# Moving modulation groups between two engines at the norm boundaries, and a reordered opening, in a two-layer diffusion backbone on one core

## The chip, the cores and the metric

The kernel runs on one core of one Trainium2 chip. The metric is the device time of one execution in microseconds (us); the time before is the median of three runs. A profiled execution was recorded beside them: its trace gives every instruction's start and length, what a waiting engine waited for, and the clock that TensorE was granted.

TensorE (PE in the profile) does the matrix products, VectorE (DVE) and ScalarE (ACT) the elementwise work, SyncE (SP) issues the DMA transfers. Each engine runs its instructions in the order in which they stand; the engines wait for each other by semaphores.

## The reference, cut to what matters

The kernel computes one step of a backbone with two layers on 640 tokens (512 latent tokens and 128 prompt tokens), model width 1024, feed-forward width 2816, in fp32. A layer is: feed-forward, mixer (even layer: retention and spatial gating; odd layer: differential attention), feed-forward. Each of these six phases starts with an RMS norm and is modulated:

```
mod = (silu(cond) @ ada_w[i] + ada_b[i]).reshape(-1, 9, 1024)[:, :, None, :]
h = modulate(rms_norm(x, norm_g[i, 0]), mod[:, 0], mod[:, 1])      # h * (1 + scale) + shift
x = x + 0.5 * mod[:, 2] * swiglu(h, ffn_w_in[i, 0], ffn_w_out[i, 0])
h = modulate(rms_norm(x, norm_g[i, 1]), mod[:, 3], mod[:, 4])
out = even_mixer(h, ...) or odd_mixer(h, ...)
x = x + mod[:, 5] * out
h = modulate(rms_norm(x, norm_g[i, 2]), mod[:, 6], mod[:, 7])
x = x + 0.5 * mod[:, 8] * swiglu(h, ffn_w_in[i, 1], ffn_w_out[i, 1])
...
return rms_norm(x, final_norm), ...
```

`swiglu` multiplies by `w_in` (1024 x 5632), takes silu(gate) times up, and multiplies by `w_out` (2816 x 1024). There are two conditions, one for the latent and one for the prompt tokens, so `mod` is a product of two vectors with a matrix of 1024 x 9216 for each layer: nine chunks of 1024 values, numbered 0 to 8.

## The kernel before, in words

**Layout.** The tokens are kept transposed: `xs` holds 8 tiles of 128 features x 640 tokens. All products work on two halves of 320 tokens, "hf 0" and "hf 1". An fp32 operand is split into a high and a low part (suffixes h and l, or `whi` and `wlo` for weights), and each 128x128 weight tile by 320 tokens takes three matmuls: high by high, low activation by high weight, high activation by low weight (lines 707, 708 and 709).

**Weights.** All weights come in groups of 1 MB, in one list called `order`, which SyncE loads one after the other into two buffers (`raw`). A buffer can be loaded again when its group has been used. For a weight group ScalarE writes `whi` (line 320) and VectorE `wlo` = raw - whi (line 321), in two pieces each. The groups are: `fin` (the feed-forward's input weights, 22 groups a phase, worked in chunks of 6, 8 and 8, and after each chunk the output weights), `fout` (four output groups after each chunk), `ein`/`eout` and `oin`/`oout` (the mixers'), and `ada` (modulation, 36 per layer, 4 per chunk). The first `NG0` `fin` groups of a phase are plain (96 matmuls), the others use Strassen's seven products (84 matmuls, with four additions on VectorE for each, lines 299 to 302, and further operand tiles that `tbuild` makes).

**Modulation groups** need no split. On TensorE a group is eight matmuls of 32x256 (`ada`, line 459, two of them joined in `order`'s rows at the opening), and a finished chunk is copied by VectorE (line 469) and turned by transposes (line 472). On VectorE a group is four multiply-and-sum passes of 128x1024 (`ada_v`, line 416 for layer 0, line 418 for layer 1). The set `ADV` lists the groups that go to VectorE. A group runs when the code comes to it in `order`: `next_group`, which fetches the next weights, runs all modulation groups that stand ahead of them (lines 395 to 397), and `mid_ada` starts a VectorE group between two steps of an output projection. The function `weave` (line 223) builds `order`: it puts one modulation group behind each weight group that isn't `fin`, and so-called pads, TensorE groups, ahead of chosen `fin` groups (`FA`).

**The norm boundary.** Where one phase ends and the next begins, the last two output groups are computed for hf 0 and then for hf 1 (`out_proj`, line 822; the odd mixer has its own version). After each product VectorE updates `xs` (line 818), ScalarE squares it (`nq`, lines 532 and 536), VectorE sums the squares (line 540). Then comes a chain for each half: TensorE sums over the features (`n?p`, line 555), VectorE computes a reciprocal square root in ten or so small instructions (from `n?m`, line 559) and spreads it on diagonals (`n?d`, line 564), TensorE broadcasts it to all partitions (`n?b`, line 567), and VectorE and ScalarE write the normed and modulated operands (`H?h`, `H?l`; in one tile with both parts `H?p`, line 626). In the names n10 to n50 the first digit is the phase that begins, the second the half. The first two `fin` groups of the next phase are computed for hf 0 first and then for hf 1 (`first_pair`, line 770). The boundaries in time: into the even mixer (about 457 us), into layer 0's second feed-forward (723), into layer 1's first (1183), into the odd mixer (1633), into layer 1's second feed-forward (1986).

**The opening.** The first norm works on the loaded `x`: ScalarE squares eight tiles, VectorE adds them up in seven additions, five matmuls of 128x1 (`n0p`, line 1553) sum over the features. Around them stand the modulation groups of chunks 0 and 1, whose results the first operands need, and warm-up matmuls (`wu`). The first two `fin` groups run in `first_wide`, whose order is a string of letters, `SQ`: a and b are modulation groups, T finishes their chunks, F readies an operand tile, W fetches the second group's weights and splits two weight pieces, G and g are products with the first and the second group.

```
SQ = 'abGTGFabGTGFWaGbGTFggggGGgggg'
    def weave(ws, ads, pads=(), fins=(), skip=()):
        ...
            if ads and w[0] != "fin" and not (w[0] == "ein" and w[1] < 2) and w[3:] not in skip:
                r.append(ads.pop(0))
    def next_group(key):
        while order[st["i"]][0] == "ada":
            next_ada()
```

## Time and profile before

| | |
|---|---|
| time before, median of 3 runs | 2453.66 us (2453.34 to 2454.06) |
| the profiled execution's own time | 2454.91 us |
| its span in the trace | 2453.1 us |
| mean granted TensorE clock | 0.991 of full speed |
| TensorE busy | 2391.2 us, 97% |
| VectorE busy | 1818.8 us, 74% |
| ScalarE busy | 1065.3 us, 43% |
| GpSimd busy | 53.0 us, 2% |
| moved by DMA | 259.32 MB, 106 GB/s on average |

The span runs from the first to the last instruction in the trace; the execution's own time lies 1.8 us above it. The busy time of an engine leaves out register, branch, semaphore and DMA-issuing instructions. In the timeline's rows the first number is the start in us, the second the length, then engine, line, operation, output and inputs; brackets hold the engine's idle time just before and what ended it. Matmuls are pipelined, so that two neighbouring ones overlap in these rows; how fast they follow each other is read from their starts.

### The profile page before, as it was taken

How to read it: one execution, taken by the hardware profiler on the slowest of the kernel's cores; microseconds unless marked ns; L12 is line 12 of the kernel's file. 1: busy time of each engine (PE TensorE's matmuls, PEld its weight loads, DVE VectorE, ACT ScalarE, POOL GpSimd, SP SyncE). 2: the span in 40 equal slices, each digit the busy share in tenths (PEclk: the TensorE clock that was granted, in tenths of full speed). 3: DMA queues.
4: the chain of work that ended last, by engine and by line, in shares of the span. 5: the costliest groups of instructions: out<-in, count | busy, mean ns of one | idle time of the engine just before them, and what ended most of it. 6: DMA issues, size and time to landing. Idle time of an engine off the chain costs nothing.

```text
span 2453.1 us, 40798 instructions
## 1 busy us (share of the span) xinstructions
PE 2391.2 (97%) x16596; PEld 2337.1 (95%) x16596; DVE 1818.8 (74%) x3723; ACT 1065.3 (43%) x2018; POOL 53.0 (2%) x82
## 2 busy tenths in 40 slices
PE   7999999999999999999999999999999999999998
PEld 6899999899999999999999999999999989999998
DVE  7677767877978777667967775779788877574664
ACT  5425345333325344243543423436767645252442
POOL 0000000000000000000000000001011000000000
PEclk9999999999999999999999999999999999999999
DMA  7332423323241423333223342332111112222121
GB/s 270 133 142 86 155 74 114 138 93 131 93 149 52 155 94 134 134 120 138 104 95 120 130 155 104 136 124 75 43 43 58 55 35 74 82 87 87 69 104 43
DMA packets 44476, 259.32 MB, mean 106 GB/s; under 512 B 5888, under 2 KB 8576, under 8 KB 16768
## 3 DMA queue, kind: packets, MB, share of 16 engines
q1 hardware_dynamic: 41024, 252.37, 28.7%
q8 instruction: 130, 2.13, 0.4%
q0 software_dynamic: 1280, 2.62, 0.3%
q10 hardware_dynamic: 1984, 1.72, 0.2%
q14 instruction: 58, 0.48, 0.1%
HBM read 252.76 MB, written 3.93 MB: 105 GB/s over the span
## 4 chain that ended last, share of the span: by engine, by line
PE 80%; DVE 10%; DMA 4%; ACT 3%; issue 1%; POOL 0%; POOLq 0%; ACTq 0%; DVEq 0%
PE op L707 8%; PE op L708 8%; PE op L709 8%; PE pu L707 7%; PE pu L709 6%; PE pu L708 6%; PE pf L707 3%; PE pf L708 3%; PE pg L709 3%; PE pf L709 3%; PE pg L707 3%; PE pg L708 3%; DVE wlo L321 3%; DMA raw<-in_w_fin 3%; ACT whi L320 2%
## 5 line engine op out<-in xcount | busy, mean ns | idle before, releaser
L321 DVE TENSOR_TENSOR wlo<-raw,whi 128x1024 fp32r<-128x1024 f32 (+1 forms) x484 | 534.0, 1119 | 297.9 <-ACT whi L320 295.8
L320 ACT ACTIVATE whi<-raw 128x1024 fp32r<-128x1024 f32 (+2 forms) x483 | 462.4, 975 | 612.2 <-PE op L708 137.9
L818 DVE SCALAR_TENSOR_TENSOR xs<-op,mod,xs 128x128 f32<-128x128 f32 (+2 forms) x312 | 124.2, 434 | 111.9 <-PE op L709 111.6
L416 DVE SCALAR_TENSOR_TENSOR raw<-raw,sb 128x1024 f32<-128x1024 f32 x72 | 87.4, 1219 | 0.6
L536 ACT ACTIVATE nq<-xs 128x320 f32<-128x320 f32 x84 | 38.6, 467 | 112.3 <-DVE xs L818 110.7
L707 PE MATMUL oq<-H4h,whi 128*128 128x320 f32 x256 | 81.1, 318 | 0.2 <-ACT ov L1015 0.2
L709 PE MATMUL oq<-H4h,wlo 128*128 128x320 f32 x256 | 79.6, 311 | 0.0
L708 PE MATMUL oq<-H4l,whi 128*128 128x320 f32 x256 | 79.3, 310 | 0.0
L1352 DVE TENSOR_REDUCE amx<-as 128x1 f32<-128x320 f32 x144 | 61.6, 460 | 19.2 <-PE as L1348 18.8
L418 DVE CUSTOM_DVE_ANT_0 raw<-raw,sb 128x1024 f32<-128x1024 f32 x60 | 72.9, 1220 | 0.7
L1360 ACT ACTIVATE ap<-as,anm 128x320 f32<-128x320 f32 x128 | 66.2, 531 | 14.1 <-DVE anm L1355 13.9
L905 ACT COPY p<-pg 128x320 f32<-128x320 f32 x76 | 32.4, 426 | 57.9 <-PE pg L709 57.8
L708 PE MATMUL pf<-H3p,whi 128*128 128x320 f32 x172 | 54.4, 318 | 1.8 <-DVE H3p L626 1.8
L708 PE MATMUL pf<-H5p,whi 128*128 128x320 f32 x172 | 53.7, 313 | 2.0 <-DVE H5p L626 2.0
L708 PE MATMUL pf<-H2p,whi 128*128 128x320 f32 x172 | 53.5, 313 | 1.8 <-DVE H2p L626 1.8
L707 PE MATMUL pf<-H3p,whi 128*128 128x320 f32 x172 | 54.5, 320 | 0.0
L709 PE MATMUL pf<-H3p,wlo 128*128 128x320 f32 x172 | 54.2, 316 | 0.0
L707 PE MATMUL pf<-H5p,whi 128*128 128x320 f32 x172 | 53.9, 317 | 0.0
L707 PE MATMUL pf<-H2p,whi 128*128 128x320 f32 x172 | 53.8, 316 | 0.0
L707 PE MATMUL pf<-H0p,whi 128*128 128x320 f32 x172 | 53.6, 314 | 0.0
L709 PE MATMUL pf<-H5p,wlo 128*128 128x320 f32 x172 | 53.4, 312 | 0.0
L301 DVE TENSOR_TENSOR raw<-raw 128x512 f32<-128x512 f32 x76 | 52.3, 688 | 1.5
(2691 smaller groups left out, 8805.0 us busy)
## 6 DMA issues: line engine op xcount, KB each, us to landing
raw<-in_w_fin SPq DMA_DIRECT2D x88, 1024.0 KB, 4.7
raw<-in_ada_w SPq DMA_DIRECT2D x64, 1024.0 KB, 4.8
raw<-in_w_fout SPq DMA_DIRECT2D x32, 1024.0 KB, 4.8
raw<-in_w_fout SPq DMA_DIRECT2D x16, 768.0 KB, 4.2
raw<-in_w_oin SPq DMA_DIRECT2D x12, 1024.0 KB, 4.8
raw<-in_w_ein SPq DMA_DIRECT2D x10, 1024.0 KB, 4.8
raw<-in_ada_w SPq DMA_DIRECT2D x32, 256.0 KB, 6.4
raw<-in_w_eout SPq DMA_DIRECT2D x4, 1024.0 KB, 4.9
```

Source lines behind the costliest of these rows:

```text
L301: sub.tensor_tensor(out=a11, in0=a22, in1=a11, op=ALU.subtract)
L320: S.activation(out=hf, in_=t, func=AF.Copy)
L321: sub.tensor_tensor(out=lf, in0=t, in1=hf.bitcast(F32), op=ALU.subtract)
L416: V.scalar_tensor_tensor(out=o, in0=w, scalar=1.0, in1=sb[:, c * D:(c + 1) * D], op0=ALU.mult, op1=ALU.mult, accum_out=r)
L418: V.tensor_tensor_reduce(out=o, in0=w, in1=sb[:, c * D:(c + 1) * D], scale=1.0, scalar=0.0, op0=ALU.mult, op1=ALU.add, accum_out=r)
L536: S.activation(out=q[:, :n], in_=x[k][:, t0:t1], func=AF.Square)
L707: PE.matmul(o, wh, xh, start=start, stop=False, skip_group_check=more)
L708: PE.matmul(o, wh, xl, start=False, stop=False, skip_group_check=more)
L709: PE.matmul(o, wl, xh, start=False, stop=stop, skip_group_check=more)
L818: V.scalar_tensor_tensor(out=x[m][:, a:b], in0=ps[:, a - t0:b - t0], scalar=mod[:, l, gmod * KD + m, c:c + 1], in1=x[m][:, a:b], op0=ALU.m ...
L1352: V.tensor_reduce(out=mx[:, j, a:a + 1], in_=sps[j][a][:, 0:w], axis=AX.X, op=ALU.max, negate=True)
L1360: S.activation(out=pj[j][:, a * 320:a * 320 + w], in_=sps[j][a][:, 0:w], func=AF.Exp, bias=b, accum_out=(sm[:, j, a:a + 1] if full else s2 ...
```

## The change

*Opening.* A new `SQ` has four new letters. h and i are the two token halves of what G did in one. s splits one weight piece (W no longer splits two). E hands the first group's sums to VectorE and ScalarE and starts `tbuild` as soon as the first group's products are done; before, that stood behind the second group's first half. `NQ = 5` leaves the squares of tiles 5, 6 and 7 out of VectorE's additions (four in place of seven); TensorE sums them, with 20 `n0p` matmuls in place of 5, and a reduction on VectorE adds the four columns. Layer 0's first feed-forward has four plain `fin` groups in place of three.

*Modulation.* Chunks 5 and 8 of layer 0, eight groups, go from VectorE to TensorE. `joined` puts four TensorE groups at the front of a phase, two ahead of its first weights and two behind its second: layer 0's chunk 5 at the even mixer, its chunk 8 at layer 0's second feed-forward, layer 1's chunk 2 at layer 1's first, and layer 1's chunk 8 at layer 1's second. The new `pe_adas` runs the first two between hf 0 and hf 1 of the last two output groups, and the other two between hf 0 and hf 1 of the new phase's first two groups. Layer 1's chunks 2 and 8 were among the pads before; `FA` shrinks from eight places to four. The `skip` list `NOA` keeps VectorE groups out of the places behind the second chunk's last output group and the third chunk's last two. At the even mixer's output, VectorE groups stand only behind the first two of four.

```diff
-NG0 = 3
-FA = (4, 8, 10, 12, 15, 16, 18, 20)
+NG0 = {(0, 0): 4, (0, 1): 3, (1, 0): 3, (1, 1): 3}
+FA = (8, 10, 15, 17)
-SQ = 'abGTGFabGTGFWaGbGTFggggGGgggg'
+SQ = 'ahbiTGFsabGTGFWaGbGsTFggggGGsEgggg'
+NQ = 5
-ADV = {(0, g) for g in range(12, 36)} | {(1, g) for g in range(24) if g // 4 != 2}
+ADV = {(l, g) for l, ms in ((0, (3, 4, 6, 7)), (1, (0, 1, 3, 4, 5))) for g in range(36) if g // 4 in ms}
...
-    l1, pl = ada_groups(1, (0, 1, 3, 4, 5)), ada_groups(1, (2, 6, 7, 8))
-    order += weave(w00[2:], ada_groups(0, [3, 4, 5]), ada_groups(0, [2]), (2, 3, 4, 5))
-    order += weave([("ein", g) for g in range(10)] + [("eout", g) for g in range(4)], ada_groups(0, [6, 7, 8]))
-    order += weave(ffn_order(0, 1), l1[:11], pl[:8], FA, ((0, 3),))
-    order += weave(ffn_order(1, 0), l1[11:], pl[8:], FA, ((0, 3),))
+    l1 = ada_groups(1, (0, 1, 3, 4, 5))
+    NOA = ((0, 3), (2, 2), (2, 3))
+
+    def joined(ws, a):
+        return a[:2] + ws[:2] + a[2:] + ws[2:]
+
+    order += weave(w00[2:], ada_groups(0, [3, 4]), ada_groups(0, [2]), (2, 3, 4, 5), NOA)
+    order += joined(weave([("ein", g) for g in range(10)], ada_groups(0, [6, 7])) + weave([("eout", g) for g in range(4)], l1[:2], skip=((2,), (3,))), ada_groups(0, [5]))
+    order += joined(weave(ffn_order(0, 1), l1[2:11], ada_groups(1, [6]), FA, NOA), ada_groups(0, [8]))
+    order += joined(weave(ffn_order(1, 0), l1[11:], ada_groups(1, [7]), FA, NOA), ada_groups(1, [2]))
     order += [("oin", g) for g in OORD] + [("oout", c, g) for c in range(2) for g in range(2)]
-    order += ffn_order(1, 1)
+    order += joined(ffn_order(1, 1), ada_groups(1, [8]))
...
+    def pe_adas():
+        while order[st["i"]][0] == "ada" and order[st["i"]][1:] not in ADV:
+            next_ada()
...
             elif c == "W":
                 W1 = next_group(keys[1])
+            elif c == "s":
                 split_piece()
-                split_piece()
-            elif c == "G":
+            elif c in "Gh":
                 assert kg < n
-                go(0, kg, W0, (0, 1))
+                go(0, kg, W0, (0, 1) if c == "G" else (0,))
+                kg += c == "G"
+            elif c == "i":
+                go(0, kg, W0, (1,))
                 kg += 1
+            elif c == "E":
+                assert kg == KD
+                yield ps, ((0, 0), (0, 1))
+                W0.done()
+                tb[0] = spawn(tbuild(0))
...
                 yield ps, 0
+                pe_adas()
...
             pe_manual((n_ == 1 or keys[0][0] == "fout") and not end)
+            if n_ == 1 and not end:
+                pe_adas()
...
-        if k:
+        if k >= NQ:
+            qs0.append(q)
+        elif k:
             V.tensor_tensor(out=acc, in0=acc, in1=q, op=ALU.add)
...
-    for b in range(5):
-        PE.matmul(ps[:, b:b + 1], acc[:, b * P:(b + 1) * P], ones[:, 0:1], start=True, stop=True)
+    for n, q in enumerate((*qs0, acc)):
+        for b in range(5):
+            PE.matmul(ps[:, 8 * b + n:8 * b + n + 1], q[:, b * P:(b + 1) * P], ones[:, 0:1], start=True, stop=True)
```

How the instructions move, at three places. The first is TensorE's order at the boundary into layer 1's first feed-forward, where hf 1 of the last two output groups (`op_1_2_2_01`) begins. Before, first the last two matmuls of hf 0 (line numbers of the kernel before):

```order
L708 MATMUL op_1_2_3_10_11824<-a0121l,whi_1_11738 128x320
L709 MATMUL op_1_2_3_10_11824<-a0121h,wlo_1_11739 128x320
L707 MATMUL op_1_2_2_01_11858<-a0114h,whi_0_11618 128x320
L708 MATMUL op_1_2_2_01_11858<-a0114l,whi_0_11618 128x320
L709 MATMUL op_1_2_2_01_11858<-a0114h,wlo_0_11619 128x320
```

Now the first pair there, and then the second pair, between the halves of the new phase's first two groups (lines 707 to 709 have become 717 to 719, line 459 is 469):

```order
L718 MATMUL op_1_2_3_10_11825<-a0121l,whi_1_11748 128x320
L719 MATMUL op_1_2_3_10_11825<-a0121h,wlo_1_11749 128x320
L469 MATMUL adaps_8_11854<-raw_11721,sc 32x256 x8
L469 MATMUL adaps_8_11854<-raw_11752,sc 32x256 x8
L717 MATMUL op_1_2_2_01_11875<-a0114h,whi_0_11628 128x320
L718 MATMUL op_1_2_2_01_11875<-a0114l,whi_0_11628 128x320
...
L719 MATMUL pf_12089<-H3p_12015,wlo_1_12188 128x320
L469 MATMUL adaps_8_11854<-raw_11981,sc 32x256 x8
L469 MATMUL adaps_8_11854<-raw_12191,sc 32x256 x8
L717 MATMUL pf_12283<-H3p_12002,whi_0_11879 128x320
L718 MATMUL pf_12283<-H3p_12002,whi_0_11879 128x320
```

Two modulation groups, 16 matmuls, now stand between the halves in each place; the boundaries into the even mixer, into layer 0's second and into layer 1's second feed-forward have the same two pairs.

The second place is VectorE at the same boundary, from the start of the first half's reciprocal square root (`n30m`) to the diagonals (`n30d`) that the broadcast waits for. Before, with one modulation pass of layer 1 (the line 418) and two subtractions (`wlo`) in the chain:

```order
L559 TENSOR_SCALAR n30m<-n30p 128x3
L418 ISA raw_11742,mod<-raw_11742,sb 128x1024
L418 ISA mod 128x1
L321 TENSOR_TENSOR wlo_0_11829<-raw_11820,whi_0_11828 128x1024
...
L321 TENSOR_TENSOR wlo_1_11961<-raw_11820,whi_1_11960 128x1024
...
L818 SCALAR_TENSOR_TENSOR xs<-op_1_2_2_11_11908,mod,xs 128x192
L818 SCALAR_TENSOR_TENSOR xs<-op_1_2_2_11_11908,mod,xs 128x128
...
L514 SCALAR_TENSOR_TENSOR n30r<-n30e,n30o 128x1 x3
L564 TENSOR_SCALAR n30d<-cst,n30r 128x128 x2
L564 TENSOR_SCALAR n30d<-cst,n30r 128x64
```

And now:

```order
L569 TENSOR_SCALAR n30m<-n30p 128x3
L327 TENSOR_TENSOR wlo_0_11880<-raw_11863,whi_0_11879 128x1024
...
L327 TENSOR_TENSOR wlo_1_11978<-raw_11863,whi_1_11977 128x1024
...
L835 SCALAR_TENSOR_TENSOR xs<-op_1_2_2_11_11928,mod,xs 128x192
L835 SCALAR_TENSOR_TENSOR xs<-op_1_2_2_11_11928,mod,xs 128x128
L524 SCALAR_TENSOR_TENSOR n30r<-n30e,n30o 128x1
L327 TENSOR_TENSOR wlo_0_11996<-raw_11873,whi_0_11995 128x1024
L524 SCALAR_TENSOR_TENSOR n30r<-n30e,n30o 128x1 x2
...
L574 TENSOR_SCALAR n30d<-cst,n30r 128x128
L574 TENSOR_SCALAR n30d<-cst,n30r 128x64
```

The modulation pass is gone, a third subtraction, on the second weight buffer (`raw_11873`), stands ahead of the diagonals, and the subtractions work on the next phase's first weights.

The third place is TensorE at the start. Before, five matmuls sum the squares between the first two modulation groups; now, twenty:

```order
L1536 MATMUL wu<-zt 128x128 x4
L1553 MATMUL n0p<-cst,nq_189 128x1 x5
L459 MATMUL adaps_0_234<-raw_0_102,sc 32x256 x2
```

```order
L1557 MATMUL wu<-zt 128x128 x4
L1578 MATMUL n0p<-cst,nq_204 128x1 x5
L1578 MATMUL n0p<-cst,nq_206 128x1 x5
L1578 MATMUL n0p<-cst,nq_208 128x1 x5
L1578 MATMUL n0p<-cst,nq_189 128x1 x5
L469 MATMUL adaps_0_246<-raw_0_102,sc 32x256 x2
```

Three rows, one for each of the squares 5 to 7, now stand ahead of the sum that VectorE has added up (`nq_189`).

26 lines of the change are left out of this document (13 added, 13 removed).

## The prediction

> **What bounds the kernel now.** I read the page's busy shares and its chain of waits first, then TensorE's timeline from end to end for its idle times, then the granted clock in short windows, and last VectorE around the waits. The page:
> ```profile
> span 2453.1 us, 40798 instructions
> PE 2391.2 (97%) x16596; PEld 2337.1 (95%) x16596; DVE 1818.8 (74%) x3723; ACT 1065.3 (43%) x2018; POOL 53.0 (2%) x82
> PE 80%; DVE 10%; DMA 4%; ACT 3%; issue 1%; POOL 0%; POOLq 0%; ACTq 0%; DVEq 0%
> ```
> TensorE sets the time. A gain must come from its instructions or from its waits; VectorE at 74% counts only where TensorE waits for it. TensorE's timeline shows where (start, duration, and in brackets the idle time before and what ended it); I leave out waits below 0.7 us and those that the change does not touch:
> ```profile
> 68.44 1.93 PE L459 MATMUL adaps<-raw,sc 128*32 128x256 f32 x32 [2.63 <-ACT a000s L939]
> 173.39 0.42 PE L707 MATMUL pg<-T00ah,whi 128*128 128x320 f32 x1 [1.47 <-ACT whi L320]
> 174.65 0.42 PE L709 MATMUL pg<-T00ah,wlo 128*128 128x320 f32 x1 [0.70 <-DVE wlo L321]
> 457.59 0.41 PE L707 MATMUL op<-a0014h,whi 128*128 128x320 f32 x1 [3.13 <-ACT whi L320]
> 458.85 0.41 PE L709 MATMUL op<-a0014h,wlo 128*128 128x320 f32 x1 [0.70 <-DVE wlo L321]
> 486.84 0.81 PE L567 MATMUL n10b<-n10d,cst 128*128 128x320 f32 x2 [1.20 <-DVE n10d L564]
> 723.22 1.41 PE L555 MATMUL n20p<-cst,nq 128*128 128x1 f32 x6 [3.57 <-DVE nq L540]
> 755.24 0.41 PE L708 MATMUL pf<-H2p,whi 128*128 128x320 f32 x1 [1.78 <-DVE H2p L626]
> 1183.77 0.81 PE L567 MATMUL n30b<-n30d,cst 128*128 128x320 f32 x2 [0.95 <-DVE n30d L564]
> 1196.00 0.80 PE L555 MATMUL n31p<-cst,nq 128*128 128x1 f32 x6 [1.55 <-DVE nq L540]
> 1210.14 0.41 PE L708 MATMUL pf<-H3p,whi 128*128 128x320 f32 x1 [1.78 <-DVE H3p L626]
> 1986.83 0.83 PE L555 MATMUL n50p<-cst,nq 128*128 128x1 f32 x6 [2.93 <-DVE nq L540]
> 2018.71 0.41 PE L708 MATMUL pf<-H5p,whi 128*128 128x320 f32 x1 [1.78 <-DVE H5p L626]
> ```
> The waits sit at the norm boundaries: I call them B1 (from 457), B2 (723), B3 (1183) and B5 (1986). B4, at about 1633, has none and the change puts nothing there. A wait costs more than its length. The first and the last of seven windows behind such waits, then one that stays fast (length, busy time, records, granted clock, DMA share, GB/s), and matmul starts at either clock:
> ```profile
> 459.90:462.90 3.00, 3.00 (x13) 0.50 0.93 322
> 2019.00:2022.00 3.00, 3.00 (x15) 0.60 0.00 0
> 70.40:74.00 3.60, 3.60 (x25) 1.00 0.93 346
> ```
> ```profile
> 26.36 0.31 PE L708 MATMUL pf<-H0p,whi 128*128 128x320 f32 x1
> 27.83 0.31 PE L709 MATMUL pf<-H0p,wlo 128*128 128x320 f32 x1
> 725.17 0.47 PE L709 MATMUL op<-sgo0h,wlo 128*128 128x320 f32 x1
> 728.90 0.47 PE L708 MATMUL op<-reo1l,whi 128*128 128x320 f32 x1
> ```
> Ten steps in 1.47 us are 0.147 us a matmul at full clock; 14 steps in 3.73 us are 0.266 at half clock. Such a stretch of 14 loses 14 x 0.119, about 1.6 us. It follows each of the seven waits of 1.55 us or more in the boundaries, no wait up to 1.47 us, and not the 2.63 us at 68.44 in the opening.
>
> So the boundaries cost now, in waits plus 1.6 us for each slow stretch: B1 3.13 + 0.70 + 1.20 + 1.6 = 6.6; B2 3.57 + 1.78 + 3.2 = 8.55; B3 0.95 + 1.55 + 1.78 + 3.2 = 7.5; B5 2.93 + 1.78 + 3.2 = 7.9. Together 30.6 us.
>
> **The change part by part.** *Work added to TensorE.* A modulation group there, with the next matmul's start, four transposes of two finished chunks, and the opening's norm sum with what starts behind it:
> ```profile
> 32.54 1.93 PE L459 MATMUL adaps<-raw,sc 128*32 128x256 f32 x32
> 34.41 0.41 PE L707 MATMUL pf<-H0p,whi 128*128 128x320 f32 x1
> 36.28 0.77 PE L472 MATMUL adaps<-cst,adac 128*128 128x128 f32 x4
> 36.80 0.39 PE L707 MATMUL pf<-H0p,whi 128*128 128x320 f32 x1
> 16.26 1.17 PE L1553 MATMUL n0p<-cst,nq 128*128 128x1 f32 x10
> 17.36 1.07 PE L459 MATMUL adaps<-raw,sc 128*32 128x256 f32 x16
> ```
> Two groups take 1.87 us, so 0.935 each, and a chunk's transposes 0.26. Sixteen groups come to four boundaries; eight of them (layer 1) leave the middles of feed-forward phases, where nothing waits, so their work is only moved. Eight (layer 0, chunks 5 and 8) come from VectorE: 8 x 0.935 + 2 x 0.26 = **+8.0 us**, and VectorE loses 32 long passes.
>
> *What goes.* At B1 the output weights came late because a VectorE group held one of the two load buffers; with none in the last output groups the 3.13 and 0.70 go, and so does their slow stretch. At B2 the 3.57 us go: VectorE's passes stood ahead of the squares, and half a row of matmuls now stands ahead of n20p. At B3 the 1.55 and at B5 the 2.93 go, for the same reasons and because two groups stand there. The three waits of 1.78 us are met by the second pair of groups, 1.87 us, which now stand between the halves; their slow stretches go too. I set the whole 30.6 us off and add what is new.
>
> *A new wait.* The groups use the same two load buffers as the weights. The next phase's first weights are requested only when TensorE has used the first group, and VectorE's subtraction on them (wlo) now stands inside the norm chain, on which the broadcast n30b waits. VectorE at B3 before, then a load and the conversion that waits for it, with the group's use at 68.44 as its trigger:
> ```profile
> 1177.07 0.16 DVE L559 TENSOR_SCALAR n30m<-n30p 128x3 f32<-128x3 f32 x1
> 1177.13 1.22 DVE L418 CUSTOM_DVE_ANT_0 raw<-raw,sb 128x1024 f32<-128x1024 f32 x1
> 1178.27 1.23 DVE L321 TENSOR_TENSOR wlo<-raw,whi 128x1024 fp32r<-128x1024 f32 x1
> 1179.55 0.48 DVE L540 TENSOR_TENSOR nq<-nq,nq 128x320 f32<-128x320 f32 x1
> 1183.07 0.64 DVE L564 TENSOR_SCALAR n30d<-cst,n30r 128x128 f32<-128x128 f32 x3
> 1987.69 0.16 DVE L559 TENSOR_SCALAR n50m<-n50p 128x3 f32<-128x3 f32 x1 [0.52 <-PE n50p L555]
> 1989.63 0.65 DVE L564 TENSOR_SCALAR n50d<-cst,n50r 128x128 f32<-128x128 f32 x3
> ...
> 69.57 0.33 SPq L267 DMA_DIRECT2D raw<-in_w_fin  x1
> 74.24 1.06 ACT L320 ACTIVATE whi<-raw 128x1024 fp32r<-128x1024 f32 x1 [2.73 <-DMA raw<-in_w_fin]
> ```
> From the first group's start: it ends at 0.94; 74.24 - 69.38 = 4.86 us later, at 5.8, the conversion starts, and at 6.9 the subtraction can. TensorE meanwhile does two groups (1.87), 24 matmuls (3.53) and n30p (0.6), so n30m runs at 6.2. The chain lasted 6.6 us, with one modulation pass (1.14) and two subtractions in it. Now it has three subtractions and one more square-add (0.4), and it waits 0.6 us for the first: 7.6 us, so n30b can start at 13.9. TensorE needs 1183.77 - 0.95 - 1176.87 = 5.95 us from n30p's end to n30b and is there at 12.0: **1.9 us of wait** at B3, and at B1 and B2, whose order reads alike. At B5 the chain was alone (1987.69 to 1990.28, 2.6 us); in it now stand three subtractions (3.4), three updates of about 0.6 and a square-add (0.4), with the 0.6 of wait 8.8 us: 3.0 us. Behind n?b on TensorE wait all matmuls; nothing else covers it. Together 8.7 us. The slow stretch followed seven of ten such waits (not the three of 1.94 to 2.63 us in the opening), so I take three of four: 4.8 us. From below, no such wait and no stretch: 0; from above, four stretches and 1 us more each: 19.1.
>
> [...]
>
> *A copy.* Each finished chunk needs one copy on VectorE in the middle of the second half's operands, just when TensorE takes them:
> ```profile
> 114.26 0.41 DVE L469 COPY adac<-adaps 128x256 f32<-128x256 f32 x1
> ```
> TensorE no longer crawls there, so I charge 0.4 four times, 1.6.
>
> *The opening.* n0p has 20 matmuls in place of 5. At (17.36 - 16.26) / 5 = 0.22 that is 3.3 us more, and a reduction adds about 0.2. TensorE reaches n0p no sooner, since its groups and warm-ups stand ahead. What follows is a VectorE chain. Ahead of the last transposes, at 47.77 now, it gets two differences (0.5 each) and loses two subtractions of 1.14 and four differences: 3.5 + 1.0 - 2.3 - 2.0 = +0.2. Behind them the second group's subtractions stand between the last operands, and TensorE waits some 1.8 us for these: +2.0. The first banks are emptied earlier, which ends the 2.63. One group is plain: 12 more matmuls, +1.8. The weights after the first chunk no longer wait for a VectorE group: -2.2 (173.39, 174.65). Sum 2.0 - 2.6 + 1.8 - 2.2 = **-1.0**, between +5.3 (the late start and the plain group stay, nothing goes) and -4.8 (the delay is absorbed, with 1.8 from the plain group).
>
> **Sum:** -30.6 + 8.7 + 4.8 + 1.6 + 8.0 - 1.0 = -8.5 us on the profiled execution's 2454.91 us (span 2453.1): 2446.4. That execution lay 1.25 us above the median, so I forecast **2445 us** against 2453.66. Its own range is 2441 to 2449.
>
> **Rivals.** (1) *The broadcast does not wait long, or the clock stays up.* For it: a wait below 1.5 us left the clock alone, 1.9 is near, and 0.6 of it hangs on the load; against it, VectorE's order puts the three subtractions there. Without stretches 2440; without waits too, -22, 2432. (2) *The late start runs through.* If the opening gives +5.3, the total is -2.2, 2451.5. For it: n0p's price is a plain row, and VectorE paces what follows. Against it: TensorE waits there already. (3) *The weights come late, and the kernel is slower.* One load here took longer:
> ```profile
> sb<-in_condb SPq DMA_DIRECT2D x1, 1024.0 KB, 6.6
> ```
> That is 1.9 us more than the usual 4.7. The first weights, then the second pair of groups, whose buffers come free only when these weights are split, would both be late at each boundary: 4 us at each of four is +16, 2461. It decides from 3.4 us a boundary on, where +13.5 turns the gain into a loss of 0.2%. Against it: the queues move little at B2, B3 and B5. (4) *The change does not do what it says:* the order shows all sixteen groups where it says, so I give it nothing.
>
> **How the numbers follow.** Forecast 0.48, (1) 0.27, (2) 0.15, (3) 0.10. The range is 2431 to 2451.5: it leaves out (3) and some of each end. A measurement of this kernel can tell 0.2%, 4.9 us, so faster means below 2448.75. Faster: 0.85 of the forecast and all of (1) and a little of (2), 0.70. Same: the rest of the forecast, most of (2), part of (3), 0.21. Slower: 0.09, nearly all (3).
>
> **What would show it.** Right: no wait above 0.7 us at n20p, n31p, n50p or the late output weights; n10b to n30b waiting about 2 us for n?d and n50b about 3, most with a window at 0.5 behind it; no 1.78 us before the second halves; n0p lasting 4.4 us; a first real matmul about 1.5 us later. Wrong: broadcasts without wait (then 1), groups or first matmuls waiting for DMA in the boundaries (then 3), or the opening's end at the first plain group 4 us later than 70.3 (then 2).

## The result, and the profile after

The changed kernel takes **2434.4 us** (median of 4 runs, 2431.29 to 2437.3) against 2453.62 us; the ratio is 0.9923, with a 95% interval of 0.9905 to 0.994. In a second set of runs it was 2433.41 us against 2454.58 us, again 0.9923 (0.9908 to 0.9939). So it is faster by 0.8%, some 19 us, where 8.7 us were forecast: the time lies in the stated range (2431 to 2451.5) and below the forecast's own range (2441 to 2449). The profiled execution took 2431.29 us with a span of 2429.5 us, 23.6 us less than the one before.

The page of the changed kernel, its busy times and the shares of its chain of waits:

```profile
span 2429.5 us, 41107 instructions
PE 2389.4 (98%) x16770; PEld 2338.1 (96%) x16770; DVE 1776.3 (73%) x3652; ACT 1063.9 (44%) x2013; POOL 54.0 (2%) x82
PE 91%; DVE 4%; ACT 2%; DMA 2%; issue 1%; POOL 0%; POOLq 0%; ACTq 0%; DVEq 0%
```

TensorE's busy time is nearly the same as before; in the chain its share went from 80% to 91%, and VectorE's from 10% to 4%. What went are waits. TensorE's timeline of the changed kernel at the places that the prediction named (columns as before; the lines 565, 577 and 469 were 555, 567 and 459):

```profile
16.05 5.77 PE L1578 MATMUL n0p<-cst,nq 128*128 128x1 f32 x40
29.41 0.42 PE L717 MATMUL pf<-H0p,whi 128*128 128x320 f32 x1
480.86 0.81 PE L577 MATMUL n10b<-n10d,cst 128*128 128x320 f32 x2 [2.10 <-DVE n10d L574]
717.65 0.72 PE L565 MATMUL n20p<-cst,nq 128*128 128x1 f32 x6
726.24 0.81 PE L577 MATMUL n20b<-n20d,cst 128*128 128x320 f32 x2 [2.04 <-DVE n20d L574]
1173.83 0.81 PE L577 MATMUL n30b<-n30d,cst 128*128 128x320 f32 x2 [2.04 <-DVE n30d L574]
1184.15 0.72 PE L565 MATMUL n31p<-cst,nq 128*128 128x1 f32 x6
1194.68 1.93 PE L469 MATMUL adaps<-raw,sc 128*32 128x256 f32 x32
1963.09 0.72 PE L565 MATMUL n50p<-cst,nq 128*128 128x1 f32 x6
1972.65 0.78 PE L577 MATMUL n50b<-n50d,cst 128*128 128x320 f32 x2 [3.01 <-DVE n50d L574]
```

The rows without brackets had no wait: n20p, n31p and n50p start at once, and the second pair of groups (1194.68) as well. The twenty sums at the start (n0p) last 5.77 us, where 4.4 were forecast. At n10b, n20b, n30b and n50b stand new waits of 2.10, 2.04, 2.04 and 3.01 us, where 1.9, 1.9, 1.9 and 3.0 were forecast. VectorE's timeline shows what they consist of, at the boundary into layer 1's first feed-forward:

```profile
1166.04 0.15 DVE L569 TENSOR_SCALAR n30m<-n30p 128x3 f32<-128x3 f32 x1
1166.80 1.23 DVE L327 TENSOR_TENSOR wlo<-raw,whi 128x1024 fp32r<-128x1024 f32 x1 [0.61 <-ACT whi L326]
1169.47 1.22 DVE L327 TENSOR_TENSOR wlo<-raw,whi 128x1024 fp32r<-128x1024 f32 x1
1171.47 1.22 DVE L327 TENSOR_TENSOR wlo<-raw,whi 128x1024 fp32r<-128x1024 f32 x1
1173.34 0.44 DVE L574 TENSOR_SCALAR n30d<-cst,n30r 128x128 f32<-128x128 f32 x2
```

Three subtractions on the next phase's weights stand in the chain, the first after a wait of 0.61 us (0.6 was forecast), and the chain from n30m to n30d lasts 7.74 us (7.6).

Where the time went, by the starts of the first halves' norm sums in the two traces. The forecast is the prediction's own, split over the same stretches; its 4.8 us for half-clock stretches stand apart:

| stretch | before, us | after, us | difference | forecast without clock | forecast clock |
|---|---|---|---|---|---|
| start to n10p | 479.09 | 472.21 | -6.9 | -4.6 | |
| n10p to n20p | 244.13 | 245.44 | +1.3 | +1.5 | +1.2 |
| n20p to n30p | 453.05 | 447.60 | -5.4 | -2.7 | +1.2 |
| n30p to n40p | 456.63 | 445.92 | -10.7 | -7.0 | +1.2 |
| n40p to n50p | 353.93 | 351.92 | -2.0 | -1.1 | |
| n50p to n60p | 452.36 | 452.48 | +0.1 | +0.5 | +1.2 |
| sum | | | -23.6 | -13.3 | +4.8 |

So 15.1 us came unforecast, for two reasons that the experiments separate: 4.8 us of half clock that this execution did not have, and 10.3 us, of which 6.4 lie between n20p and n40p, where two feed-forward phases run.

### The profile page after: what moved, and what is told of

Same layout as the page of the kernel before. It is cut to its first block, busy times and chain, and to the rows that moved or that the text cites. A ratio compares the mean times of both kernels' runs of the same rounds, so it can differ in the third digit from the quotient of the medians.

```text
span 2429.5 us, 41107 instructions
## 1 busy us (share of the span) xinstructions
PE 2389.4 (98%) x16770; PEld 2338.1 (96%) x16770; DVE 1776.3 (73%) x3652; ACT 1063.9 (44%) x2013; POOL 54.0 (2%) x82
## 3 DMA queue, kind: packets, MB, share of 16 engines
q8 instruction: 131, 2.15, 0.3%
q10 hardware_dynamic: 1984, 1.72, 0.2%
## 4 chain that ended last, share of the span: by engine, by line
PE 91%; DVE 4%; ACT 2%; DMA 2%; issue 1%; POOL 0%; POOLq 0%; ACTq 0%; DVEq 0%
PE op L718 9%; PE op L717 9%; PE op L719 9%; PE pu L717 7%; PE pu L719 7%; PE pu L718 7%; PE pf L717 4%; PE pf L719 4%; PE pf L718 4%; PE pg L719 4%; PE pg L718 4%; PE pg L717 4%; PE oq L717 1%; PE atb L1422 1%; PE oq L718 1%; DVE wlo L327 1%
## 5 line engine op out<-in xcount | busy, mean ns | idle before, releaser
L717 PE MATMUL pf<-H0p,whi 128*128 128x320 f32 x200 | 63.0, 317 | 0.0
L719 PE MATMUL pf<-H0p,wlo 128*128 128x320 f32 x200 | 62.3, 312 | 0.5 <-DVE wlo L327 0.5
L718 PE MATMUL pf<-H0p,whi 128*128 128x320 f32 x200 | 62.0, 311 | 0.0
L426 DVE SCALAR_TENSOR_TENSOR raw<-raw,sb 128x1024 f32<-128x1024 f32 x48 | 58.3, 1220 | 0.5
```

Of the source, the lines that this page charges most:

```text
L426: V.scalar_tensor_tensor(out=o, in0=w, scalar=1.0, in1=sb[:, c * D:(c + 1) * D], op0=ALU.mult, op1=ALU.mult, accum_out=r)
L717: PE.matmul(o, wh, xh, start=start, stop=False, skip_group_check=more)
L718: PE.matmul(o, wh, xl, start=False, stop=False, skip_group_check=more)
L719: PE.matmul(o, wl, xh, start=False, stop=stop, skip_group_check=more)
```

## The experiments

The sets ran on different chips; each kernel is compared with the kernel before on its own chip, or with a kernel of its own set. The runs of one kernel scatter over 2 to 13 us here; the first experiment shows why.

### The half clock: the changed kernel again

No edit; a second profile. In the two profiles so far the granted clock changes between 1.00 and 0.50, ahead of the last microseconds in half-clock stretches of 3.41 and 6.83 us: six and two of them in the kernel before, one and two in the changed kernel.

> The changed kernel once more, for a second profile. Its four times so far fall in two groups, 2431.3 and 2432.3 us at a mean granted clock of 0.994, 2437.3 and 2436.5 us at 0.992. Grid theory: TensorE's clock is decided for one window of 3.41 us after the other, and a wait halves it only where most of the wait falls into one window. In the profile at 2431.3 us all four waits for n?d (2.0 to 3.0 us) lie across a border of two windows, and none is followed by half clock; in an execution near 2437 us three of the four would be followed by half clock, 3.41 us each, at 1.7 us each. So: times between 2430 and 2438 us again; where the profile lies high it shows such stretches behind n?b, where low none, with waits of the same length. Rival, duration theory: such waits don't halve the clock at all, and the 5 us come from elsewhere, such as later loads.

Measured: 2433.41 us (2430.65 to 2442.46). The waits at n?b were the same as in the first profile (2.01, 2.05, 2.10 and 2.96 us), and this time one of the four was followed by half clock. The row of that wait, and windows of this second profile at the last half-clock stretch of the opening and around the wait (length, busy times, granted clock, DMA share, GB/s):

```profile
1173.52 1.44 PE L577 MATMUL n30b<-n30d,cst 128*128 128x320 f32 x2 [2.10 <-DVE n30d L574]
```
```profile
43.10:43.50 0.40, 0.15 (x1) 0.15 (x2) 0.40 (x2) 0.00 (x0) 0.00 (x0) 1.00 0.00 0
43.60:46.90 3.30, 3.30 (x15) 3.22 (x14) 2.84 (x12) 1.20 (x3) 0.00 (x0) 0.50 0.85 285
1171.42:1173.30 1.88, 0.00 (x0) 0.00 (x0) 1.88 (x7) 0.26 (x1) 0.00 (x0) 1.00 0.83 288
1173.40:1176.70 3.30, 3.18 (x10) 2.79 (x11) 1.60 (x5) 1.02 (x2) 0.00 (x0) 0.50 0.32 134
1176.80:1178.80 2.00, 2.00 (x16) 2.00 (x15) 1.91 (x5) 0.91 (x2) 0.00 (x0) 1.00 0.00 0
```

And the same two places in the first profile of the changed kernel:

```profile
43.00:46.30 3.30, 3.22 (x13) 3.18 (x14) 2.71 (x12) 1.14 (x3) 0.00 (x0) 0.50 0.91 303
1171.80:1173.80 2.00, 0.00 (x0) 0.00 (x0) 1.98 (x7) 0.19 (x1) 0.00 (x0) 1.00 0.81 311
1173.90:1176.10 2.20, 2.20 (x14) 2.04 (x15) 1.24 (x3) 0.84 (x2) 0.00 (x0) 1.00 0.38 160
```

The half clock begins at 43.53 and at 1173.34 us in the second profile (the exact borders are those at which the granted clock changes in the trace). These are 1129.8 us apart, which is 331 times 3.4133 us. The traces of the two kernels show the same step: ahead of the last microseconds their half-clock stretches begin 132, 77, 10, 129, 4, 228 and 9 times 3.4133 us apart in the kernel before, and 3 and 7 times in the changed kernel. I call such a step a window. In the first profile the borders lie differently against the program: from 42.96, 331 windows on, a border falls on 1172.77, into the middle of the wait (1171.79 to 1173.83), 0.98 us before it and 1.06 behind. In the second profile 1.92 us of the wait lie in one window. So at n30b the wait of 2.10 us that lies mostly in one window was followed by half clock, and the one of 2.04 us that a border halves was not; what differs between the two executions is where the borders fall.

### The half clock: everything 0.9 us later

```diff
+SHIFT = 7
...
+        if (l, md) == (0, 2):
+            for _ in range(SHIFT):
+                PE.transpose(ps[:, 256:256 + P], c[:, 0:P], ident)
```

> Seven more 128x128 transposes on TensorE in chunk 2 of layer 0, which repeat one that is there: about 0.9 us more work at about 110 us, so that everything behind it comes 0.9 us later. Grid theory: the waits at n10b, n20b, n30b and n50b lie 0.9 us further in their windows, 1.9 us or more of each in one window, and each stretch that follows moves the next wait by 1.7 us more, about half a window, to the other side: all four are followed by a half-clock window of 3.41 us, and the time is 0.9 + 4 x 1.7 = 7.7 us above a run of the changed kernel without stretches (2439 us), and at the least two of the four. Duration theory: 0.9 us more and no half clock behind the waits (2432 us).

Measured: 2440.16 us (2435.49 to 2446.2), 6.75 us above the second set's changed kernel; the profile took 2436.96 us. Two of the four waits were followed by a window of half clock, n10b and n50b. The parts that lie in one window were 1.91 and 2.15 us there, 1.37 and 1.75 at the two others (n20b, n30b). So the part in one window tells the waits apart here too, but my count of four failed. I had counted on a shift of 0.9 us against the borders of the first profile; the borders lay nearly the same here (one at 43.05 us, there at 42.96), but the edit cost more than its 0.9 us, since one product waited 1.75 us at 126.03 us where none had waited. The 6.75 us are therefore no clean test of the size; the parts in the windows are.

Taking all ten profiles of this study that have waits of 2 to 4 us at n?b together, 34 waits: 16 were followed by half clock. The largest part in one window without half clock behind it was 1.85 us (n50b in the first profile of the changed kernel), the smallest with it 1.91 us. By the granted clock of 0.50 a window of half clock costs half of its 3.41 us, 1.7 us, while TensorE has work; that is an estimate, and by the steps between products, 0.267 us in such a window of the first profile and 0.147 outside, it is 1.5. The duration theory is out: waits of 2.0 to 2.2 us stood on both sides.

### The opening: three kernels

NQ alone, the squares back on VectorE:

```diff
-NQ = 5
+NQ = 8
```

> The changed kernel with the first norm's squares all added up on VectorE (NQ 8 in place of 5): five n0p matmuls in place of twenty. In the profile n0p began at 16.05 us as before, and the chain behind it 4.4 us later than before (21.86 against 17.47), while VectorE had stood idle for 9.6 us. Theory that the late start runs through: the first chunk is paced by VectorE behind the chain, the start comes about 4 us earlier and the whole is 3 to 4.4 us shorter than the changed kernel. Rival, that the opening absorbs it: TensorE or the loads set the pace by the end of the first groups, the whole is within 1 us of the changed kernel.

Measured: **2427.55 us** (2426.63 to 2435.09), 5.9 us less than the changed kernel of its set; lowest against lowest 4.0 us. A repeat in the last set was 2428.54 us. VectorE's timeline of the changed kernel, and then VectorE's and TensorE's with NQ 8, at the norm sum and at the first product:

```profile
21.86 0.18 DVE L1582 TENSOR_REDUCE n0m<-n0p 128x5 f32<-128x20 f32 x1 [9.58 <-PE n0p L1578]
```
```profile
17.30 0.17 DVE L1582 TENSOR_REDUCE n0m<-n0p 128x5 f32<-128x5 f32 x1 [2.22 <-PE n0p L1578]
23.29 0.41 PE L717 MATMUL pf<-H0p,whi 128*128 128x320 f32 x1
```

VectorE waited 9.58 us for TensorE's sums. With five sums in place of twenty its chain starts 4.6 us earlier and the first product 6.1 us (23.29 for 29.41), and 4 to 6 us of this reach the end. The late start runs through. In the profiles n10p starts 7.7 us earlier (464.55 for 472.21), but n10b then waits 3.86 us in place of 2.10, with two windows of half clock behind it, and 3.7 us are left at the end.

The twenty sums also cost more than their number. Windows of TensorE in the changed kernel, while they run and behind:

```profile
16.10:19.00 2.90, 2.90 (x29) 2.90 (x28) 0.00 (x0) 0.00 (x0) 0.00 (x0) 1.00 0.95 350
19.10:25.80 6.70, 6.70 (x40) 5.41 (x40) 2.82 (x16) 1.33 (x2) 0.00 (x0) 0.50 1.04 371
```

TensorE is busy with 128x1 matmuls for 2.90 of 2.90 us, and yet half clock follows, for two windows. In five of the six profiles with twenty sums such a stretch begins among them, between 18.45 and 19.64 us, and in the sixth one that began at 10.63 lasts through them; in the eight with five sums there is none between 17 and 30 us. This fits the 5.77 us: 20 matmuls at 0.22 us are 4.4, and those behind 19.07 us take about twice as long (the trace has 9 of their 40 records in the 1.70 us from 20.10, and 19 in the 2.00 us from 16.05).

The old opening in the changed kernel (SQ, NQ, the plain groups and the code of the letters as before, the rest as changed):

```diff
-NG0 = {(0, 0): 4, (0, 1): 3, (1, 0): 3, (1, 1): 3}
+NG0 = {(0, 0): 3, (0, 1): 3, (1, 0): 3, (1, 1): 3}
-SQ = 'ahbiTGFsabGTGFWaGbGsTFggggGGsEgggg'
-NQ = 5
+SQ = 'abGTGFabGTGFWaGbGTFggggGGgggg'
+NQ = 8
...
+    split_piece()
+    tb[0] = spawn(tbuild(0))
```

> The changed kernel with the opening of before (SQ, NQ 8, three plain groups, the place of the first operands' T tiles), the rest as changed (2433.4 us here). By the prediction the opening was worth 1.0 us, of which 2.2 us come from the loads behind the first chunk, which stay: so 2432 us (1.2 us less than the changed kernel). Late-start theory: the new opening begins 3.3 us later with its first product and was at the third chunk's output groups 1.7 us ahead of before, so its other parts gain about 4 to 5 us: with the old opening 2434 to 2435 us, and 7 us or so more than with NQ 8 in the new opening (2427.6).

Measured: 2432.31 us (2429.7 to 2436.66), ratio 0.9918 (0.9893 to 0.9942) against the changed kernel's 0.9923: no difference that these runs can tell. It is 4 to 5 us above NQ 8 in the new opening (2427.55 and 2428.54, other chips); the intervals of the ratios overlap (0.9884 to 0.9911 and 0.9882 to 0.9919 there), but the traces agree: n10p starts at 471.46 us here and at 464.55 and 463.90 there, and TensorE's waits of 1.39, 1.21 and 1.00 us at 68.77, 116.11 and 122.58 stand in the old opening alone.

The new opening alone in the kernel before:

```diff
-NG0 = 3
-SQ = 'abGTGFabGTGFWaGbGTFggggGGgggg'
+NG0 = {(0, 0): 4, (0, 1): 3, (1, 0): 3, (1, 1): 3}
+SQ = 'ahbiTGFsabGTGFWaGbGsTFggggGGsEgggg'
+NQ = 5
...
```

The code of the letters and of the sums goes with it, as in the change.

> The kernel before with the new opening alone (SQ, NQ 5, four plain groups); groups, places and boundaries as before (2454.6 us here). By the prediction +1.2 us (2.0 for the late start, -2.6 for the wait at 68 us, +1.8 for the plain group), since the waits at 173 us stay: 2455.8 us. If the opening's other parts gain 4 to 5 us against the 3.3 us of late start and the 1.8 us of the plain group: 2454 to 2455 us. Either way the opening carries none of the 20 us; if this kernel is 5 us or more faster, it does.

Measured: 2453.2 us (2447.32 to 2460.18), ratio 1.0006 (0.9991 to 1.0022), 1.3 us above the kernel before; 1.2 were predicted, within what the runs can tell. What follows from the three: the opening carries none of the 19 us, as far as these runs can tell. Its reordered products gain 4 to 5 us, and the twenty sums give these back.

### The waits at n?b: three kernels that move something out of the chain

First, the broadcast later in TensorE's order:

```diff
-NB = (9, 9)
+NB = (16, 9)
```

> The changed kernel with the broadcast of each first half (n10b to n50b) placed 16 steps of three matmuls behind its diagonals in place of 9, so 21 matmuls (3.1 us) later in TensorE's order. Theory that the three weight subtractions in the norm chain are what the four waits consist of, and that nothing behind the broadcast is as late: the waits of 2.0, 2.0, 2.0 and 3.0 us go, and with them any half clock behind them: 9 us less than an execution of the changed kernel without stretches, up to 14 less than one with three (2422 us). Rival: the operands that need the broadcast come 3 us later too, and TensorE waits for them at the first products of the next phase: as long as before, 2431 us or more.

Measured: 2463.17 us (2460.44 to 2470.88), ratio 1.0046 (1.003 to 1.0061): 30 us above the changed kernel of its set. The waits at n10b to n30b are gone (n50b keeps 2.56 us), and longer ones stand at the operands that hang on the broadcast, with half clock behind them (the profile's mean granted clock is 0.986, and 0.993 in the changed kernel's of its set). TensorE's timeline:

```profile
738.08 0.70 PE L577 MATMUL n20b<-n20d,cst 128*128 128x320 f32 x2
759.26 0.63 PE L717 MATMUL pf<-H2p,whi 128*128 128x320 f32 x1 [4.04 <-ACT H2p L631]
1211.63 0.41 PE L717 MATMUL pf<-H3p,whi 128*128 128x320 f32 x1 [4.05 <-ACT H3p L631]
```

Second, with NQ 8, VectorE's order written out, with the subtractions behind the diagonals:

```diff
+                if n_ == 1 and not end and nxt != 4:
+                    la[0] = 0 if gi == 2 else 2
+                    if gi == 2:
+                        dm = tc.manual_schedule(engines={mybir.EngineType.DVE})
+                        dm.__enter__()
...
+            if n_ == 1 and not end and nxt != 4:
+                dm.__exit__(None, None, None)
...
```

The odd mixer's own output projection gets the same lines.

> The changed kernel with NQ 8 (2427.6 us, 2426.6 at the lowest), and VectorE's order written out while hf 1 of the last two output groups runs (at the four boundaries that have groups): the subtractions on the next phase's first weights come behind the diagonals n?d, in place of ahead of them and between the steps of the chain. No work is added or left out. Theory that the subtractions in the norm chain are what n?b waits for: the chain lasts as long as that at the second halves (n31m to n31d, 3 us), the waits of 2.0 to 3.9 us at n10b, n20b, n30b and n50b go, and since the operands start about 2 us earlier, nothing new is late: 9 us less and the half-clock windows behind them too, 2416 to 2419 us. Rival, that VectorE as a whole is the bound there: the subtractions come later, so the first products of the next phase or the second pair of groups wait for them or for the loads behind them, as when the broadcast was moved: 2426 us or more.

Measured: 2430.01 us (2428.77 to 2431.08), no gain over NQ 8. TensorE's timeline:

```profile
1167.20 0.70 PE L577 MATMUL n30b<-n30d,cst 128*128 128x320 f32 x2
1175.83 0.41 PE L719 MATMUL pf<-H3p,wlo 128*128 128x320 f32 x1 [1.46 <-DVE wlo L327]
1180.81 0.80 PE L565 MATMUL n31p<-cst,nq 128*128 128x1 f32 x6 [0.56 <-DVE nq L550]
```

All four waits at n?b are gone, so they do consist of the subtractions. But between n30b and n31p the 2.2 us come back and 1 us more: the first products now wait for the same subtractions. The rival is right here: behind the norm sum VectorE is the bound, and moving work within that stretch gains nothing. What is left is to take work out of the stretch.

Third, with NQ 8, the first pair of groups seven microseconds earlier, so that the next weights are requested earlier:

```diff
                     Ws[gi] = next_group(keys[gi])
+                    if gi == 3 and not end:
+                        pe_adas()
```

> The changed kernel with NQ 8, and the first pair of groups at the boundaries into phases 1, 2 and 3 seven microseconds earlier: ahead of the last output group's hf 0, in place of between hf 0 and hf 1. No work is added or left out. Their loads landed some 8 us before their use in the profile, VectorE then stood idle for 1.9 us four times and for 4.0 us, and the next phase's first weights were requested only when the pair was used. Theory that the late request is what puts the subtractions into the norm chain: one subtraction now falls into VectorE's idle time ahead of the chain, the others behind n?d, the waits at n10b, n20b and n30b go (2.0 to 2.2 us each, with the half-clock windows behind them), and nothing else is later: 6.2 to 9 us less than NQ 8 alone, about 2420 us. Rival, that VectorE as a whole is the bound there, as with the subtractions put behind the chain: the gain comes back as waits at the first products, 2426 us or more.

Measured: **2418.22 us** (2417.67 to 2424.57), 10.3 us less than NQ 8 on the same chip (2428.54), and 0.9864 of the kernel before (0.9848 to 0.988): the best kernel of this study, 34 us under the kernel before. The loads of the next weights, as SyncE's queue issues them, in the changed kernel and here, and then VectorE and TensorE with the early pair:

```profile
1160.89 1.19 SPq L273 DMA_DIRECT2D raw<-in_w_fin  x2
```
```profile
1142.46 1.80 SPq L273 DMA_DIRECT2D raw<-in_w_fin  x2
1148.60 1.22 DVE L327 TENSOR_TENSOR wlo<-raw,whi 128x1024 fp32r<-128x1024 f32 x1 [1.03 <-ACT whi L326]
1154.65 0.15 DVE L569 TENSOR_SCALAR n30m<-n30p 128x3 f32<-128x3 f32 x1
1156.92 0.65 DVE L574 TENSOR_SCALAR n30d<-cst,n30r 128x128 f32<-128x128 f32 x3
1160.25 0.70 PE L577 MATMUL n30b<-n30d,cst 128*128 128x320 f32 x2
1958.96 1.41 PE L577 MATMUL n50b<-n50d,cst 128*128 128x320 f32 x2 [2.97 <-DVE n50d L574]
```

Against n30m the request comes 12.2 us earlier here and 5.2 us earlier in the changed kernel. One subtraction now falls into VectorE's idle time ahead of the chain, the chain from n30m to n30d lasts 2.9 us in place of 7.7, and n30b doesn't wait, nor do n10b and n20b. The odd mixer's boundary was left as it was and keeps its 2.97 us. So the late request was the cause of three of the four waits.

### The groups: in the middle of the phases, at the boundaries, left out

The sixteen boundary groups spread over their phases, one ahead of each of the input weights 2 to 5:

```diff
-        return a[:2] + ws[:2] + a[2:] + ws[2:]
+        r, a = [], list(a)
+        for w in ws:
+            if w[0] in ("fin", "ein") and 2 <= w[-1] <= 5:
+                r.append(a.pop(0))
+            r.append(w)
+        assert not a
+        return r
```

> The changed kernel, but the sixteen groups that stand at the boundaries run in the middle of the phases, one ahead of each of the input weights 2 to 5 (opening, ADV and the skipped places as in the changed kernel, 2433.4 us here). At the boundaries no engine has a group now. Theory of the prediction: the second pair of groups is what covers the wait for the second half's first operands, so the three waits of 1.78 us (H2p, H3p, H5p) come back, each with an even chance of a half-clock window behind it (1.7 us); the first weights are loaded early again and are split ahead of the chain, so the four waits at n?b (9.2 us) go; n20p, n31p and n50p stay without long waits, since half a row of matmuls or none was needed there only because of VectorE's groups. Sum 5.3 + 2.5 - 9.2 - 3.4 (two half-clock windows) = -5 us: 2428 us. Rival: the groups at the boundary also end the waits at n31p and n50p (1.55 and 2.93 us before), and a group in the middle of a phase costs more than the 0.93 us that it lasts: 2434 us or more.

Measured: 2446.12 us (2444.45 to 2449.25), ratio 0.9973 (0.9961 to 0.9985): 12 to 13 us above the changed kernel (2433.4 and 2434.4 us, other chips). Rows of TensorE's timeline:

```profile
718.09 0.80 PE L571 MATMUL n20p<-cst,nq 128*128 128x1 f32 x6 [0.45 <-DVE nq L556]
747.30 0.42 PE L724 MATMUL pf<-H2p,whi 128*128 128x320 f32 x1 [0.59 <-DVE H2p L642]
808.34 0.41 PE L725 MATMUL pg<-T20ah,wlo 128*128 128x320 f32 x1 [1.21 <-DVE wlo L333]
1182.87 0.72 PE L571 MATMUL n31p<-cst,nq 128*128 128x1 f32 x6
1193.40 1.07 PE L475 MATMUL adaps<-raw,sc 128*32 128x256 f32 x16
1195.40 0.42 PE L724 MATMUL pf<-H3p,whi 128*128 128x320 f32 x1 [0.59 <-DVE H3p L642]
1970.97 1.44 PE L571 MATMUL n50p<-cst,nq 128*128 128x1 f32 x6 [2.93 <-DVE nq L556]
```

Four readings. First, the boundaries aren't free of groups, against what was expected: `pe_adas` still finds the group of the input weights 2 at the head of `order` and runs it between the halves of the first two groups (1193.40). The waits at the second halves come back as 0.59 us, not as 1.78, and this one group is why: TensorE needs 1.20 us for it (worked out below), and 1.20 + 0.59 is 1.79. From n31b to the operand the time is the same, 6.15 us before and 6.14 here. So the second pair, 2.06 us, does cover the 1.78. Second, at n20p 0.45 us come back and at n31p nothing, without a group of TensorE ahead of them: there the pair isn't needed, and the skipped places are what is left of the change. Only n50p's 2.93 us need the first pair. Third, all four waits at n?b are gone, n50b's too, so they come with the first pair. Fourth, the kernel is slower nevertheless: layer 0's second feed-forward takes 89.0 us from its first product to its first output product, in place of 83.3 in the changed kernel, with two groups more in it. Four single groups are 4.8 us there where the pair was 2.06, and 2.6 us are waits behind them (0.59, 0.81 and the 1.21 us for wlo).

What such a group costs, with NQ 8 as the base: four of the eight groups that stay in the middle left out, and the same four loaded but with one matmul of eight.

```diff
-FA = (8, 10, 15, 17)
+FA = (8, 17)
...  ada_groups(1, [6])[::3] ... ada_groups(1, [7])[::3]
```
```diff
-        for k in range(KD):
+        for k in range(1 if l == 1 and md in (6, 7) and q in (1, 2) else KD):
```

> The changed kernel with NQ 8 once more, as the kernel that the other three of this set are compared with: 2427 to 2429 us, as before (2427.6).

> The changed kernel with NQ 8, without four of its eight TensorE groups in the middle of the phases: groups 1 and 2 of layer 1's chunks 6 and 7 are left out altogether, loads and matmuls (the modulation is incomplete, the rest of the work the same). By the prediction's price a group is its matmuls, 0.93 us: 3.7 us less (2424 us). If a group in the middle also keeps one of the two load buffers from the weights and so costs 1.8 to 1.9 us, as the two traces of the phases say: 7.2 to 7.6 us less (2420 us).

> The changed kernel with NQ 8, with the same four groups loaded, but with one matmul of their eight (seven are left out). If the price of a group in the middle is its matmuls, 4 x 0.82 = 3.3 us less, and the four left out altogether would give little more. If half of the price is the load buffer, which a group still takes here, 3.3 us less here and 7 or more without the groups.

Measured: the base 2428.54 us; without the four groups **2420.64 us** (2418.52 to 2426.27), 7.9 us less; with their loads but nearly without their matmuls 2430.42 us (2427.13 to 2435.16), 1.9 us more. The stretches in which the four stand, from a chunk's first product to its first output product in the three traces:

| chunk | base | without groups | loads only |
|---|---|---|---|
| layer 0, second feed-forward, second chunk | 101.5 | 99.9 | 101.0 |
| the same, third chunk | 101.9 | 100.0 | 103.0 |
| layer 1, first feed-forward, second chunk | 102.4 | 100.0 | 100.9 |
| the same, third chunk | 102.1 | 100.0 | 102.6 |
| sum, us | 407.8 | 399.9 | 407.5 |

A group costs 2.0 us there. TensorE's rows at one of the four show a part of it, first in the base and then with loads only:

```profile
902.98 0.31 PE L719 MATMUL pu<-T23bh,wlo 128*128 128x320 f32 x1
903.22 1.07 PE L469 MATMUL adaps<-raw,sc 128*32 128x256 f32 x16
904.47 0.31 PE L718 MATMUL pu<-H2p,whi 128*128 128x320 f32 x1
```
```profile
906.15 0.31 PE L719 MATMUL pu<-T23bh,wlo 128*128 128x320 f32 x1
906.39 0.62 PE L469 MATMUL adaps<-raw,sc 128*32 128x256 f32 x2
907.19 0.31 PE L718 MATMUL pu<-H2p,whi 128*128 128x320 f32 x1
```

From the matmul ahead of the group to the second one behind it, two steps that take 0.29 us where no group stands, it is 1.49 us in the base: the group takes 1.20 us of TensorE's time. It is the same at each of the base's eight single groups, and a pair at a boundary takes 2.06. The first step to the group and the first two behind it are longer than the steps within (0.24, 0.31 and 0.25 us for 0.147), and they stay when seven of the eight matmuls are left out: 1.04 us, so 0.75 for the group. I had counted on 0.82 us less for each and got 0.45, together 1.8 us, of which 0.3 are left in the sum. The rest went into waits for the next weights in the two third chunks, 1.18 us (row below) and 1.14:

```profile
1056.10 0.41 PE L719 MATMUL pg<-T20ah,wlo 128*128 128x320 f32 x1 [1.18 <-DVE wlo L327]
```

So of the 2.0 us of a group 1.20 are TensorE's own time and 0.8 short waits behind it. With the load in place, less TensorE time brought next to nothing; in the two second chunks it brought 0.5 and 1.4 us, in the two third ones it cost 1.1 and 0.5. That the load alone is the price is not shown, since no run has the matmuls without the load. (The loads-only kernel's profiled execution is 3.3 us longer than the base's, and that is half clock: five windows of it behind n?b against three, by the estimate 1.7 us each; the mean granted clock is 0.993 for 0.995.)

## Why the prediction was right or wrong

**The direction, and the 30.6 us at the boundaries: right.** Every wait of the prediction's list is gone from the first profile of the changed kernel, but those at n10b and n30b, where the forecast put new ones. The reason for the second halves holds: one group of 1.20 us in place of the pair leaves 0.59 of the 1.78 us. For n50p the first pair is what ends the wait, as forecast. At n31p it wasn't needed: without it no wait came back. That VectorE's groups made the output weights late at 457 us was not tested alone.

**The new wait: right, in place, mechanism and size.** 2.10, 2.04, 2.04 and 3.01 us for 1.9, 1.9, 1.9 and 3.0. The late request as its cause was shown by the early pair, which takes the waits away at three boundaries, and the subtractions by the written order, which takes away all four.

**The half clock, +4.8 us: the wrong kind of number.** I took three of four waits, from seven of ten in one trace. The first profile of the changed kernel had none of four, the second had one, all ten together 16 of 34, so about half, near 3 us on average. The cause that the prediction lacked is the windows of 3.4133 us, 331 of them in the 1129.8 us of the second profile: at n?b a wait was followed by half clock where 1.91 us or more of it lay in one, and not where 1.85 us or less did.

**The copies, +1.6 us:** in the changed kernel's trace no matmul waits for an operand in the second halves behind them, so nothing of the 1.6 us shows there. They were not measured alone.

**The opening, -1.0 us: right within what the runs tell, its parts not.** The chain came 4.4 us later (21.86 for 17.47) and the first product 3.3 us, where 3.5 and 1.5 were forecast, and NQ 8 shows that this start runs through, as the second rival has it. The prediction's 0.22 us a sum left out the half clock, which began among the twenty sums in five profiles of six and among five sums in none of eight. The reordered products gain as much: beside the 2.63 us wait, those of 1.21 and 1.04 us at 115.86 and 122.38 are gone, which the prediction didn't list.

**The step that failed** is the sentence that layer 1's eight groups "leave the middles of feed-forward phases, where nothing waits, so their work is only moved". I priced a group at 0.935 us wherever it stands, half the time from the first start in a pair to the start of the next matmul. That leaves out the slower steps around it: a pair takes 2.06 us and a single group 1.20, and in the middle some 0.8 us of waits behind it come on top, 2.0 us in all. At a boundary the change's groups run without a wait. In the two feed-forward phases that held the groups, the second and third chunks together took 418.9 us before and 408.1 after, 10.7 us less for six groups less, 1.8 us each, where 5.6 us were forecast. Six times 1.20 are 7.2 us; the other 3.5 are waits behind the groups, and the runs don't separate these from VectorE's groups, which the change also moves. The 5.1 us above the forecast are half of the 10.3 that were missing. Of the rest, 2.3 us lie ahead of n10p and 2.9 us in the other stretches; I haven't traced these to single waits.

**The rivals.** The first (no waits at n?b, or no half clock, 2432 or 2440 us) is near the measured time, but its mechanism is only half there: the waits came, and the half clock comes or not by the execution. So it is luck that its 2432 us lies so near: the profiled execution came there by having no half clock at n?b and by 10.3 us that no rival had, about half of them the groups' price. The second (late start) is true of the start and not of the sum. The third (weights late, slower) didn't occur: the second pair and the first products start without a wait for DMA.

## What to carry to other kernels

Price a piece of work by what a stretch takes with it and without it, and not by its own instructions: here eight small matmuls, 0.935 us by their rows in a pair, took 1.20 us of TensorE's time alone between others, and 2.0 us with the waits behind them. Leaving out seven of the eight while the load stayed gained next to nothing. Where a wait is made of work that another engine does too late, look for that engine's idle time further ahead, and move the request there; moving the wait, or the work within the bound stretch, gave nothing or cost 30 us. A cost that comes by chance, as the half clock here (behind 16 of 34 waits), belongs into a range as a probability for each wait, and two profiles of the same kernel tell more about it than one.

## What was not expected of the hardware

Ahead of the last microseconds TensorE's granted clock changed, in the traces of the two kernels and at both places read from the second profile, only at borders of a grid of 3.4133 us, and a half-clock stretch of the two lasted one window or two, 3.41 or 6.83 us. Against the program the grid lay differently in two executions of the changed kernel: a stretch began at 42.96 us in the first and at 43.53 us in the second. At n?b a wait was followed by half clock from 1.91 us in one window on, and not up to 1.85. What decides in other places stays open: in the kernel before, waits of 1.78 us that lay in one window were followed by half clock three times of three, and one of 1.55 us ahead of the 128x1 sums too, while one of 1.72 us in one window was not (1475.46 in the trace with the shift). And it began among twenty 128x1 sums in a row, without any wait, in five traces of six. So the length of a wait alone doesn't tell whether half clock follows, and what does tell it the runs here don't show.
